# Moving the first input sums, the fetches behind them and the last prepared weights of a one-core decoder layer

## The chip, the cores and the metric

The kernel runs on one core of a Trainium2 chip. The core has a matrix engine (TensorE, PE in the rows; PEld is its weight load), a vector engine (VectorE, DVE), a scalar engine (ScalarE, ACT), a general engine (GpSimd, POOL) and SyncE (SP), which only issues transfers. Each engine works through its own list of instructions in order and waits on semaphores for the others. Transfers are put on a queue by SP, ACT or POOL and run beside the engines.

The metric is the device time of one execution in microseconds (us), the median over several runs. Before the change it is 2637.97 us over three runs (2630.3, 2637.97 and 2639.31).

## What is computed

One decoder layer on 1024 tokens of width 1024, in float32. Only the first of its four parts is touched by most of the change:

```
h = x
f = swiglu(rmsnorm(h, ffn1_pre_g), ffn1_w_gu, ffn1_w_down)   # first feed-forward
h = h + 0.5 * rmsnorm(f, ffn1_post_g)
m = hybrid_mixer(rmsnorm(h, mix_pre_g), ...)                  # attention heads beside a state-space scan
h = h + rmsnorm(m, mix_post_g)
c = memory_cross_attention(rmsnorm(h, xa_pre_g), ...)
h = h + rmsnorm(c, xa_post_g)
f = swiglu(rmsnorm(h, ffn2_pre_g), ffn2_w_gu, ffn2_w_down)   # second feed-forward
h = h + 0.5 * rmsnorm(f, ffn2_post_g)

def swiglu(h, w_gu, w_down):
    g, u = jnp.split(h @ w_gu, 2, axis=-1)
    return (jax.nn.silu(g) * u) @ w_down
```

`D_FF` is 2816, that is 22 column blocks of 128 for the gate and 22 for the up half of `w_gu`.

## The kernel before

**Precision.** A float32 product is made of three matmuls. Each operand is split into a high part (a cast on ACT, L274) and a low part (the rest, a subtraction on DVE, L276), and `mm3` adds high by high, high by low and low by high (L139). So every weight tile costs ACT a cast and DVE a subtraction before TensorE can use it.

**The way up** (`up_phase`). The tokens stand in two halves of 512 columns. The first three gate and up blocks (f = 0 to 2) are plain projections of 24 matmuls each. From f = 3 on, `seven(f)` computes gate and up of both halves at once as seven block products of 12 matmuls each (Strassen's scheme in Winograd's form), 84 matmuls for each f, 19 times. The seven products need sums of input quarters and sums of weight quarters.

- *Input sums.* For k = 0 to 3, `fetch(k)` loads two pairs of quarter rows of x with four transfers on POOL's queue (L686): the pair "ad" into `raw2` (two buffers) and the pair "bc" into `blk`. `steps(k)` then scales the first pair on ACT (L689) and makes three sums on DVE (L699, L702) with their splits (L274, L276) into the tiles S1, S4 and S5. The third load into `raw2` can start only when the sums of k = 0 have read theirs. After these come the differences `B21` (`below`) and `B12` (`again`, `differ`, `last`, L742), which take their data from further loads on POOL's queue.
- *Weight sums.* `pieces(f)` makes five sums of weight quarters on POOL (L762, tile `wc`) and splits seven blocks. For f = 3 each of the five sums is kept in program order.
- *Results.* ACT and DVE take each finished product out of PSUM (L818 to L848); `act_sums` and `pair_sums` make the sums of activations that the way down needs; `act_sums` loads stored activations back over POOL's queue (L621) and adds them on DVE (L628).

**Prepared weights** (`prepare`). Weights of the mixer are split ahead of time while TensorE is busy with the way up. A piece is half a weight tile: one load of 256 KB, a cast on ACT (L212), a subtraction on DVE (L216) and two stores of 256 KB (L226). `prepare_all` queues 64 pieces, those of 20 tiles `ssd` and of the first `QKV` = 12 tiles `qkv`. Fifty-nine of them have times 4100 ns apart from 148000 on and use SP's queue; the last five have times 9000 ns apart from 446000 on, and their loads and stores stand on POOL's queue. The rest of `qkv` (from tile `QKV` on) is prepared in the state-space stage.

**The way down** (`down7`). Again seven block products, over 11 blocks of the contraction, 132 matmuls each. For each block SP loads a weight block (L1018, L1023) and an activation block (L1029), DVE makes a sum (L1032) and splits both (L276). At the end of a product DVE and ACT take the four banks out of PSUM (L1054, L1089) before the next product can add to them.

**What sets the order.** TensorE's order is the program's. Work of the other engines that is not tied to a matmul is put on a list, `self.later`, with a planned time; it is emitted when the planned clock, the sum of the estimated matmul costs, passes this time. What goes through `kp` stays in program order on its engine. The rest a scheduler orders by estimated times and by priority; `urgent` lifts priority. In the running program each engine's list is fixed: an instruction that waits holds back all behind it on the same engine or queue.

Of the kernel before, what the change touches and what calls it, by code (L numbers as in the profile page):

```python
# [10 lines left out]
F32 = mybir.dt.float32  # L11
# [12 lines left out]
NFF = 22  # L24
PLAIN = 3, 4
MIXED = 6
QKV = 12
MEM = 256
EPS = 1e-6

# [17 lines left out]
class Kern:  # L48
# [139 lines left out]
        self.split(hi, lo, raw)  # L188
        return hi, lo

    def prepare(self, names, raw, pairs, times, switch=float("inf")):


        nc = self.nc
        work = []
        for name, i in names:
            hl = tuple(self.tc.dram_tile([P, KT, P], F32R, name=self.nm(n)) for n in ("dwhi", "dwlo"))
            self.ready[name, i] = hl
            work += [(self.ap["w_" + name][i], hl, slice(4 * n, 4 * n + 4)) for n in range(2)]
        raws, parts = {}, {}  # L200

        def queue(n):
            return nc.sync if times[n] < switch else nc.gpsimd

        def load(n):
            pool, tag, bufs = raw[n % len(raw)]
            raws[n] = self.t(pool, [P, 4, P], F32, tag, bufs=bufs)
            self.kp(queue(n).dma_start(out=raws[n], in_=work[n][0][:, work[n][2], :]))

        def high(n):  # L210
            parts[n] = [self.t(pool, [P, 4, P], F32R, tag, bufs=bufs) for pool, tag, bufs in pairs[n % len(pairs)]]
            self.kp(nc.scalar.copy(parts[n][0], raws[n]))  # L212

        def low(n):
            hi, lo = parts[n]
            self.kp(nc.vector.tensor_tensor(out=lo, in0=raws.pop(n), in1=hi.bitcast(F32), op=ALU.subtract))  # L216

        def st0(n):
            store(n, 0)

        def st1(n):
            store(n, 1)

        def store(n, i):
            d, x = work[n][1][i], parts[n][i]
            self.kp(queue(n).dma_start(out=d[:, work[n][2], :].bitcast(F32), in_=x.bitcast(F32)))  # L226

        if len(pairs) > 2:
            steps = ((low, -1, 0), (st0, -2, 0), (st1, -2, 3000), (high, 0, 0), (load, 2, 6000))
        else:  # L230
            steps = ((high, 0, 0), (low, 0, 1200), (load, 2, 2400), (st0, 0, 3000), (st1, 0, 3000))
        times = list(times)[: len(work)]
        assert len(times) == len(work), (len(times), len(work))
        d = times[1] - times[0]
        times = {n: t for n, t in enumerate(times)}
        times.update({-n: times[0] - d * n for n in (1, 2)})
        times.update({len(work) + n: times[len(work) - 1] + d * (n + 1) for n in range(2)})
        for n in sorted(times):
            for f, m, dt in steps:
                if len(pairs) > 2 and times[n] < switch:  # L240
                    dt = 0
                if 0 <= n + m < len(work):
                    self.later.append((times[n] + dt, lambda f=f, m=n + m: f(m)))

# [4 lines left out]
    def prepare_all(self, sp):  # L249
        names = [("ssd", i) for i in [*range(6), *range(12, 26)]] + [("qkv", i) for i in range(QKV)]  # L250
        pairs = [
            ((self.fp, "acc0", None), (self.fp, "acc1", None)), ((self.fp, "rpost", None), (self.tp, "dg", None)),
            ((sp, "bh", None), (sp, "bl", None)),
        ]
        raw = [(sp, "braw", 2), (sp, "braw", 2), (self.xp, "xl0", KT + 1), (self.xp, "xl1", KT + 1)]
        n = 2 * len(names)
        a = [148000 + 4100 * i for i in range(n)]
        k = sum(t < 388000 for t in a)
        self.prepare(names, raw, pairs, a[:k] + [446000 + 9000 * i for i in range(n - k)], 418000)

    def wsrc(self, name, i):
        return self.ready[name, i] if (name, i) in self.ready else self.ap["w_" + name][i]
# [306 lines left out]
    def up_phase(self, sp, sp2, wgu, gpre, act_d, bank, load, plain, sizes, rw=None, begin=None):  # L569

        nc = self.nc
        NFT, NWC, NBLK = sizes
        first_seven = PLAIN[0 if begin else 1]
# [8 lines left out]
        if begin:  # L582
            x = sums(F32)
# [163 lines left out]
        def at(t, f, *args):  # L747
            self.later.append((t, lambda: f(*args)))


        def pieces(f):

            G, U = (load(wgu[2 * f + i], [P, KT, P]) for i in range(2))
# [2 lines left out]
            for a, b, op in (  # L756
# [3 lines left out]
                if b is not None:  # L760
                    t = self.t(sp if begin else sp2, [P, 4, P], F32, "wc", bufs=NWC)
                    inst = nc.gpsimd.tensor_tensor(out=t, in0=a, in1=b, op=op)  # L762
                    if begin and f == first_seven:
                        self.tc.keep_in_program_order(inst)
                    a = t
                n = self.nblk = (self.nblk + 1) % (6 + NBLK)
# [101 lines left out]
            )):  # L868
                homes["ca", k] = homes["bd", k] = x
        for k in range(4):  # L870
            at(t0 + dt * k, fetch, k)
            for n, f in enumerate(steps(k)[: 4 if begin else 5]):
                at(t0 + dt * (k + 1) + 1500 * n, f)

        def gate(w, hh):
            t, ps = ft(), self.proj_now(w, hh)
# [10 lines left out]
        if begin:  # L887
# [10 lines left out]
            for hh in range(2):  # L898
# [6 lines left out]
                t = ts[hh]  # L905
# [1298 lines left out]
    def run(self):  # L2204
        nc, tc, ap = self.nc, self.tc, self.ap
        with tc.tile_pool(name="const", bufs=1) as cp, tc.tile_pool(name="state", bufs=1, reuse_waits="tile") as xp, \
# [54 lines left out]
            def begin(step):  # L2261
                if step < 0:
                    warm()
                elif step == 0:
                    load_x(0)
                elif step == 1:
                    consts()
                    norm_x(0, 8500, 13500)
                else:
                    load_x(1)  # L2270
                    norm_x(1, 22000, 25500)

            self.kv_d = [[tc.dram_tile([P, 4, MEM], F32R, name=f"kv{h}{n}") for n in range(2)] for h in range(4)]
            self.h = [[ap["xT"][d, :, hh * H : (hh + 1) * H] for d in range(KT)] for hh in range(2)]
# [110 lines left out]
```

## Time and profile before

| | before |
|---|---|
| median of three runs | 2637.97 us (2630.3 to 2639.31) |
| profiled execution, its own time | 2634.21 us |
| its span | 2632.4 us |
| mean granted TensorE clock | 0.994 of full speed |
| DVE busy | 1990.6 us (76%) |
| ACT busy | 1291.9 us (49%) |
| POOL busy | 589.4 us (22%) |
| read from and written to memory | 466.4 MB, 177 GB/s over the span |

The profiled execution is one execution of the same program under the profiler; its span is the part between the first and the last instruction. Shares of the span say little here: TensorE is busy nearly always. What matters is the few places at which it isn't, and for each the instruction that it waits for and what stands ahead of that one on its engine.

### The profile page before, as it was taken

Reading aid. Unit: us, or ns where it says so; the run is one execution under the profiler, and the core shown is the slowest. Engines: PE = TensorE matmul, PEld = TensorE weight load, DVE = VectorE, ACT = ScalarE, POOL = GpSimd, SP = SyncE. Lnnn points to the kernel's source line nnn. Section 1 sums busy time; section 2 is a strip of 40 time slices with the busy share of each in tenths; the row PEclk is TensorE's granted clock in tenths of the full one; section 3 lists DMA queues with packets and bytes.
Section 4 is the critical chain, followed back from the end, with each engine's and each line's share of the span. In section 5 each row is a group of like instructions: output and inputs, shape, how many; then the busy total and the mean of one; then the engine's idle time right before and its main releaser. Section 6 shows DMA issues by size and latency. Waiting matters only on the chain.

```text
span 2632.4 us, 36830 instructions
## 1 busy us (share of the span) xinstructions
PE 2586.2 (98%) x12850; PEld 2153.1 (82%) x12850; DVE 1990.6 (76%) x3044; ACT 1291.9 (49%) x2300; POOL 589.4 (22%) x696
## 2 busy tenths in 40 slices
PE   9899999989999999999999999999999999999999
PEld 7688888878777778888888897888878888888887
DVE  6778887768779875777777787767566888777777
ACT  6434443545356664555555555346554433333553
POOL 2555554010100001111111110101011555552000
PEclk9899999999999999999999999999999999999999
DMA  6458887664655516555555556537658453326554
GB/s 227 162 179 293 288 285 259 220 224 142 241 204 188 180 58 207 164 163 141 149 138 134 168 155 230 195 137 248 211 172 294 158 176 116 101 96 228 188 172 152
DMA packets 214314, 489.82 MB, mean 186 GB/s; under 512 B 26544, under 2 KB 35120, under 8 KB 214128
## 3 DMA queue, kind: packets, MB, share of 16 engines
q1 hardware_dynamic: 165920, 374.98, 43.1%
q0 software_dynamic: 24880, 70.01, 8.8%
q10 hardware_dynamic: 23328, 42.48, 4.3%
q8 instruction: 101, 1.65, 0.3%
q14 instruction: 85, 0.70, 0.1%
HBM read 327.46 MB, written 138.94 MB: 177 GB/s over the span
## 4 chain that ended last, share of the span: by engine, by line
PE 86%; DVE 6%; DMA 2%; issue 2%; ACT 2%; POOL 0%; SPq 0%; DVEq 0%; ACTq 0%; POOLq 0%
PE mm L139 45%; PE dn L139 33%; PE z L139 2%; PE tr L142 2%; PE y L139 1%; PE ms L142 1%; PE ms L139 1%; PE seg L139 1%; DMA oraw<-mix 1%; DVE nb L1771 1%; DVE wlo L276 1%; DMA raw<-in_w_dn 1%; PE st L139 0%; DVE xl L276 0%; DVE whi L276 0%
## 5 line engine op out<-in xcount | busy, mean ns | idle before, releaser
L139 PE MATMUL mm<-xh,whi 128*128 128x512 f32 x1320 | 522.1, 405 | 6.8 <-DVE whi L276 2.8
L139 PE MATMUL mm<-xh,wlo 128*128 128x512 f32 x1272 | 488.9, 392 | 0.0
L139 PE MATMUL mm<-xl,whi 128*128 128x512 f32 (+1 forms) x1252 | 487.3, 389 | 1.2 <-DVE xl L276 0.9
L139 PEld LDWEIGHTS mm<-xh,whi 128*128 128x128 f32 x1320 | 249.1, 189 | 49.4 <-issue 3.8
L139 PEld LDWEIGHTS mm<-xh,wlo 128*128 128x128 f32 x1272 | 239.1, 188 | 52.4 <-DVE wlo L276 0.4
L139 PEld LDWEIGHTS mm<-xl,whi 128*128 128x128 f32 x1252 | 236.5, 189 | 35.6 <-DVE xl L276 1.8
L1771 DVE TENSOR_TENSOR_SCAN nb<-nb,begin 128x128 f32<-128x128 f32 (+7 forms) x128 | 171.5, 1352 | 52.1 <-ACT nb L1767 51.6
L1767 ACT ACTIVATE nb<-z,scale 128x128 f32<-128x128 f32 (+2 forms) x192 | 107.8, 580 | 77.7 <-PE z L139 77.5
L276 DVE TENSOR_TENSOR wlo<-wraw,whi 128x1024 fp32r<-128x1024 f32 x70 | 85.5, 1221 | 54.8 <-ACT whi L274 48.4
L274 ACT CAST whi<-wraw 128x1024 fp32r<-128x1024 f32 (+1 forms) x87 | 83.8, 964 | 81.1 <-PE mm L139 55.2
L1788 POOL DMA_DIRECT2D mix<-sq x64 | 52.8, 825 | 228.6 <-DVE sq L1786 176.2
L670 ACT ACTIVATE ft<-ft 128x512 f32<-128x512 f32 x88 | 55.5, 632 | 96.1 <-DVE ft L669 95.5
L139 PE MATMUL dn<-xh,wlo 128*128 128x512 f32 x296 | 101.4, 390 | 0.6 <-DMA wlo<-dwlo 0.6
L762 POOL TENSOR_TENSOR wc<-raw,wraw 128x512 f32<-128x512 f32 x55 | 79.4, 1443 | 57.9 <-DVE blk L276 22.8
L762 POOL TENSOR_TENSOR wc<-wraw,raw 128x512 f32<-128x512 f32 x56 | 79.4, 1418 | 51.0 <-DVE whi L276 15.9
L276 DVE TENSOR_TENSOR atl<-tr,ath 128x512 fp32r<-128x512 f32 (+1 forms) x108 | 67.9, 632 | 30.0 <-ACT ath L274 29.6
L849 POOL TENSOR_TENSOR ft<-ft,e 128x512 f32<-128x512 f32 x37 | 59.8, 1616 | 121.4 <-DVE e L848 53.5
L139 PE MATMUL mm<-ath,v 128*128 128x256 f32 x320 | 85.9, 291 | 0.4 <-ACT sq L1785 0.2
L274 ACT CAST ath<-tr 128x512 fp32r<-128x512 f32 (+1 forms) x108 | 58.8, 546 | 55.4 <-PE tr L142 51.0
L139 PE MATMUL dn<-xh,blk 128*128 128x512 f32 x264 | 85.2, 389 | 0.0
L139 PE MATMUL dn<-hl,whi 128*128 128x512 f32 x288 | 76.0, 397 | 9.1 <-ACT F L1089 9.1
L274 ACT CAST wlo<-wc 128x512 fp32r<-128x512 f32 x79 | 49.1, 621 | 71.3 <-PE dn L139 21.9
(586 smaller groups left out, 6799.4 us busy)
## 6 DMA issues: line engine op xcount, KB each, us to landing
whi<-dwhi SPq DMA_DIRECT2D x82, 512.0 KB, 3.6
wlo<-dwlo SPq DMA_DIRECT2D x82, 512.0 KB, 4.8
wraw<-in_w_gu SPq DMA_DIRECT2D x43, 512.0 KB, 4.0
dwhi<-bh SPq DMA_DIRECT2D x75, 256.0 KB, 4.1
dwlo<-bl SPq DMA_DIRECT2D x75, 256.0 KB, 4.0
raw<-in_w_gu SPq DMA_DIRECT2D x37, 512.0 KB, 4.2
wraw<-xs SPq DMA_DIRECT2D x56, 256.0 KB, 3.0
xs<-ft ACTq DMA_DIRECT2D x54, 256.0 KB, 3.8
```

Source lines behind the costliest of these rows:

```text
L139: self._pe(self.nc.tensor.matmul(out, lhsT, rhs, start=start, stop=stop, skip_group_check=self.more), cost)
L142: self._pe(self.nc.tensor.transpose(out, src, self.ident if ident is None else ident), 109.0)
L274: self.kp(self.nc.scalar.copy(hi, src))
L276: self.nc.vector.tensor_tensor(out=lo, in0=src, in1=hi.bitcast(F32), op=ALU.subtract)
L670: nc.scalar.activation(t, t, AF.Silu)
L762: inst = nc.gpsimd.tensor_tensor(out=t, in0=a, in1=b, op=op)
L849: nc.gpsimd.tensor_tensor(out=t1, in0=t1, in1=e, op=ALU.mult)
L1767: nc.scalar.activation(nb[:, s0:s1], z[:, 0:n], AF.Sigmoid, scale=sc[:, i : i + 1])
L1771: nc.vector.tensor_tensor_scan(out=nb[:, 0:Wd][:, ::-1], data0=nb[:, 0:Wd][:, ::-1], data1=begin[:, S - Wd : S][:, ::-1], initial=0.0, op0 ...
L1788: nc.gpsimd.dma_start(out=self.mix_d[p][a * 64 : a * 64 + 64, csl], in_=o, accum_op=ALU.add)
```

## The change

Five edits.

1. `steps(0)`, the scaling and the three sums of the first pair, is emitted with raised priority (`soon`) and with times from 5000 ns behind its fetch on, 300 ns apart.
2. The fetches for k = 1 to 3 get the planned offsets 7000, 8000 and 13500 in place of 6000, 12000 and 18000, and their steps 9500, 17000 and 23000 in place of 12000, 18000 and 24000. The two small matmul groups of the second half's norm move to the planned times 24000 and 27500, from 22000 and 25500.
3. Of the five weight sums of f = 3 only the first, `G0 + G1`, is kept in program order.
4. All prepared pieces have times 3900 ns apart from 148000 on and use SP's queue; there are no late pieces and no pieces on POOL's queue. The two stores of a piece stand in one step.
5. `QKV` is 11, so `prepare_all` has 62 pieces, and the two pieces of `qkv` tile 11 go to the state-space stage, in front of the 24 that are there.

```diff
-QKV = 12
+QKV = 11
...
-    def prepare(self, names, raw, pairs, times, switch=float("inf")):
+    def prepare(self, names, raw, pairs, times):
...
-        def queue(n):
-            return nc.sync if times[n] < switch else nc.gpsimd
...
-            self.kp(queue(n).dma_start(out=raws[n], in_=work[n][0][:, work[n][2], :]))
+            self.kp(nc.sync.dma_start(out=raws[n], in_=work[n][0][:, work[n][2], :]))
...
-        def store(n, i):
-            d, x = work[n][1][i], parts[n][i]
-            self.kp(queue(n).dma_start(out=d[:, work[n][2], :].bitcast(F32), in_=x.bitcast(F32)))
+        def store(n):
+            for d, x in zip(work[n][1], parts.pop(n)):
+                self.kp(nc.sync.dma_start(out=d[:, work[n][2], :].bitcast(F32), in_=x.bitcast(F32)))
 
         if len(pairs) > 2:
-            steps = ((low, -1, 0), (st0, -2, 0), (st1, -2, 3000), (high, 0, 0), (load, 2, 6000))
+            steps = ((low, -1, 0), (store, -2, 0), (high, 0, 0), (load, 2, 0))
...
-                if len(pairs) > 2 and times[n] < switch:
-                    dt = 0
...
-        a = [148000 + 4100 * i for i in range(n)]
-        k = sum(t < 388000 for t in a)
-        self.prepare(names, raw, pairs, a[:k] + [446000 + 9000 * i for i in range(n - k)], 418000)
+        self.prepare(names, raw, pairs, [148000 + 3900 * i for i in range(n)])
...
+        def now(f):
+            f()
+
+        def soon(f):
+            with self.urgent():
+                f()
...
-                    if begin and f == first_seven:
+                    if begin and f == first_seven and a is G0 and b is G1:
                         self.tc.keep_in_program_order(inst)
...
         for k in range(4):
-            at(t0 + dt * k, fetch, k)
+            t, u, d = (t0 + dt * k, t0 + dt * (k + 1), 1500)
+            if begin:
+                t, u, d = ((0, 5000, 300), (7000, 9500, 1000), (8000, 17000, 1500), (13500, 23000, 1500))[k]
+                t, u = t0 + t, t0 + u
+            at(t, fetch, k)
             for n, f in enumerate(steps(k)[: 4 if begin else 5]):
-                at(t0 + dt * (k + 1) + 1500 * n, f)
+                at(u + d * n, soon if begin and k == 0 else now, f)
...
-                    norm_x(1, 22000, 25500)
+                    norm_x(1, 24000, 27500)
```

The edits shift the lines: rows of the kernel before at L699, L702, L276, L348 and L376 stand at L686, L689, L263, L335 and L363 in the changed one, POOL's weight sums (L762) at L756, its other work (L823, L849) at L817 and L843, and the residual loads (L389) at L376.

DVE's list in the first 50 us, before, from the place right behind the sums of squares of the second half's norm (`acc`, none of which stands below) and the first sum of k = 0, `bl_492`. `bh_506` and `bl_517` are the other two sums of k = 0, `S` the splits of all three, `wlo` splits of plain weight tiles, `cpre` the norm of the second half, `ft` gate values.

```order
L276 TENSOR_TENSOR wlo_661<-wraw_658,whi_660 128x1024
L348 RECIPROCAL cpre_112_346<-cpre_112_346 128x4
L276 TENSOR_TENSOR S_116_361<-bl_492,S_116_361 128x512
L276 TENSOR_TENSOR wlo_667<-wraw_664,whi_666 128x1024
L669 TENSOR_TENSOR ft_463<-mm_464,rpre_113_347 128x512
L702 SCALAR_TENSOR_TENSOR bh_506<-blk_441,params_78,raw_134_438 128x512
L884 TENSOR_TENSOR ft_463<-ft_463,mm_503 128x512
L276 TENSOR_TENSOR S_120_365<-bh_506,S_120_365 128x512
L702 SCALAR_TENSOR_TENSOR bl_517<-blk_441,params_78,raw_134_438 128x512
```

The changed kernel, from the first sum of k = 0 (`bl_476`) to the first plain weight split:

```order
L686 TENSOR_TENSOR bl_476<-raw_134_438 128x512
L363 TENSOR_TENSOR acc_104_323<-acc_104_323,sq_108_334 128x512
L363 TENSOR_TENSOR acc_104_323<-acc_104_323,sq_109_337 128x512
L263 TENSOR_TENSOR S_116_361<-bl_476,S_116_361 128x512
L689 SCALAR_TENSOR_TENSOR bh_481<-blk_441,params_78,raw_134_438 128x512
L363 TENSOR_TENSOR acc_104_323<-acc_104_323,sq_110_340 128x512
L363 TENSOR_TENSOR acc_104_323<-acc_104_323,sq_111_343 128x512
L263 TENSOR_TENSOR S_120_365<-bh_481,S_120_365 128x512
L689 SCALAR_TENSOR_TENSOR bl_486<-blk_441,params_78,raw_134_438 128x512
L263 TENSOR_TENSOR wlo_663<-wraw_660,whi_662 128x1024
L335 RECIPROCAL cpre_112_346<-cpre_112_346 128x4
```

All three sums of k = 0 now stand ahead of the weight split `wlo` and ahead of the gate values `ft_463`; the last of them, the last reader of the first `raw2` buffer, no longer stands behind two results of TensorE. The sums of squares of the second half now stand between them, the last ones three places later than before.

POOL's list in the way down, before. The `dwhi` and `dwlo` stores belong to the last of the late pieces (five loads and eight more stores of such pieces stand above), the loads of L389 fetch the residual of the first half.

```order
L226 DMA dwhi_656<-bh_5043 128x512
L226 DMA dwlo_657<-bl_5044 128x512
L226 DMA dwhi_656<-acc_1147_5123 128x512
L226 DMA dwlo_657<-acc_1148_5124 128x512
L389 DMA xl_1243_5651<-in_xT 128x512
L389 DMA xl_1248_5680<-in_xT 128x512
```

POOL's list in the changed kernel around the same residual loads (now L376); `sq` and `ft` are the last work of the way up.

```order
L843 TENSOR_TENSOR ft_4149<-ft_4149,e_4103 128x512
L817 TENSOR_TENSOR sq_941_4201<-sq_941_4201,sq_940_4200 128x512
L843 TENSOR_TENSOR ft_4291<-ft_4291,e_4263 128x512
L376 DMA xl_1235_5633<-in_xT 128x512
L376 DMA xl_1240_5662<-in_xT 128x512
```

No transfer of a prepared piece is left between the last work of the way up and the loads of the residual. On DVE's list the late subtractions (L216) between the sums of the way down are gone likewise; the rows around them keep their order, but for two pairs of neighbours that change places.

More of the change, by code (lines that the diff above doesn't have):

```diff
@@ L216, in low @@
             self.kp(nc.vector.tensor_tensor(out=lo, in0=raws.pop(n), in1=hi.bitcast(F32), op=ALU.subtract))
[L218 to L222, printed above, removed]
-        def store(n, i):
-            d, x = work[n][1][i], parts[n][i]
-            self.kp(queue(n).dma_start(out=d[:, work[n][2], :].bitcast(F32), in_=x.bitcast(F32)))
+        def store(n):
+            for d, x in zip(work[n][1], parts.pop(n)):
+                self.kp(nc.sync.dma_start(out=d[:, work[n][2], :].bitcast(F32), in_=x.bitcast(F32)))
         if len(pairs) > 2:
-            steps = ((low, -1, 0), (st0, -2, 0), (st1, -2, 3000), (high, 0, 0), (load, 2, 6000))
+            steps = ((low, -1, 0), (store, -2, 0), (high, 0, 0), (load, 2, 0))
         else:
-            steps = ((high, 0, 0), (low, 0, 1200), (load, 2, 2400), (st0, 0, 3000), (st1, 0, 3000))
+            steps = ((high, 0, 0), (low, 0, 1200), (load, 2, 2400), (store, 0, 3000))
         times = list(times)[: len(work)]
```

## The prediction

> **What bounds the kernel now.** I read the page first, then who waits for whom on PE, then a table of stretches, then PE's order of time at the places that these name.
>
> ```profile
> span 2632.4 us, 36830 instructions
> PE 2586.2 (98%) x12850; PEld 2153.1 (82%) x12850; DVE 1990.6 (76%) x3044; ACT 1291.9 (49%) x2300; POOL 589.4 (22%) x696
> PE dn L139 <- ACT F L1089: 9.1, 1, 9.1
> PE mm L139 <- DVE e L828: 5.4, 2, 4.7
> PE mm L139 <- DVE whi L276: 2.8, 1, 2.8
> ```
>
> PE is the bound. The change neither adds nor removes a matmul, so all it can win is time in which PE stands still or runs slowly. The first line of the page gives 2632.4 - 2586.2 = 46 us of idle PE; three waits of one instance each make up 16.6 us of it. The stretches of 10 us (us; then busy time and instructions of PE, PEld, DVE, ACT, POOL; granted clock; DMA share; GB/s) show where:
>
> ```profile
> 80.00:90.00 10.00, 6.22 (x17) 4.29 (x15) 5.60 (x7) 2.21 (x5) 4.87 (x5) 0.68 0.38 132
> 100.00:110.00 10.00, 9.21 (x39) 7.33 (x40) 10.00 (x13) 3.54 (x6) 6.29 (x5) 1.00 0.02 4
> 120.00:130.00 10.00, 5.34 (x16) 3.97 (x15) 6.70 (x11) 1.85 (x3) 3.47 (x4) 0.73 0.75 256
> 240.00:250.00 10.00, 10.00 (x45) 8.27 (x45) 10.00 (x14) 4.22 (x8) 5.96 (x4) 1.00 0.73 232
> 550.00:560.00 10.00, 3.06 (x7) 2.49 (x8) 5.66 (x10) 3.09 (x6) 0.00 (x0) 0.56 0.53 194
> ```
>
> A full stretch holds 45 matmuls; these hold 17, 39, 16 and 7. Between 140 and 540 us PE is full throughout, as at 240, even where DVE is. So there are three holes: at 81 to 102 and 121 to 132 (start of the seven products) and at 548 to 562 (way down). The change touches all three.
>
> **First hole, the sums in front.** PE's order of time (start, duration) and the chain of waits (the two with a count at the end):
>
> ```profile
> 81.63 0.50 PE L139 MATMUL mm<-xh,whi 128*128 128x512 f32 x1 [1.00 <-ACT whi L274]
> 85.14 1.22 PE L139 MATMUL mm<-xh,whi 128*128 128x512 f32 x2 [2.77 <-DVE whi L276]
> 102.33 2.89 PE L139 MATMUL dn<-S,wlo 128*128 128x512 f32 x12
> 147.95 8.16 PE dn L139 x36
> 85.14 4.65 PE mm L139 x10
> ```
>
> Undisturbed matmuls come every 8.16 / 36 = 0.227 us. PE was free at 81.63 - 1.00 = 80.63; five products, 60 matmuls, later it is at 102.33, and 60 x 0.227 = 13.6, so 8.1 us are lost here. What is late is DVE:
>
> ```profile
> 46.40 0.74 DVE L702 SCALAR_TENSOR_TENSOR bl<-blk,params,raw 128x512 f32<-128x512 f32 x1
> 47.69 1.06 POOL L686 DMA_DIRECT2D raw<-in_xT  x2 [31.25 <-DVE bl L702]
> 65.80 0.69 DVE L276 TENSOR_TENSOR S<-bl,S 128x512 fp32r<-128x512 f32 x1 [3.07 <-ACT S L274]
> 83.81 0.68 DVE L884 TENSOR_TENSOR ft<-ft,mm 128x512 f32<-128x512 f32 x1
> 84.40 1.28 DVE L276 TENSOR_TENSOR whi<-wc,whi 128x512 fp32r<-128x512 f32 x2
> 90.95 0.69 DVE L276 TENSOR_TENSOR wlo<-wc,wlo 128x512 fp32r<-128x512 f32 x1 [5.26 <-ACT wlo L274]
> ```
>
> The third sum of k = 0 ran at 46.40; POOL's next loads waited 31 us for it, so the data for k = 2 came late; DVE stood for 3.07 us at 65.8 and then reached L884 at 83.81, 3.2 us after PE had its operand ready, and the low half of the first block behind it.
>
> With the change that third sum stands in front of the weight split and the gate values. Counting DVE's new list on from the gate product ahead of it (about 32.0 before) with 0.69 to 0.74 us each and the casts between, it ends near 39, 8 us earlier, and the loads for k = 2 follow. The sums of k = 1 stay where results of PE hold them, so k = 3 gains only about 1 us of its load. The 3.07 us at 65.8 go, since k = 2's data are there and the cast for S now stands ahead of the scaling that waited for a load. I put DVE at the gate product of 83.81 some 3 us sooner, that is when PE delivers (about 81.1). The low half then ends near 82.3; PE waits some 1.2 us instead of 1.00 + 2.77, and isn't slowed after it. The end of the first product moves from 89.8 to 84.7, and with it ACT's read of that bank, the cast behind it and DVE's split at 90.95: 5 us. From there DVE is busy without a break to 115 us (the row 100 to 110 shows 10.00), so everything behind moves by these same 5 us, no more.
>
> *The clock* has its share in this. The ten matmuls after the second wait took 4.65 us, 0.465 each, twice 0.227: 2.4 us on top of the wait; the granted clock of that stretch is 0.68.
>
> **Second hole.**
>
> ```profile
> 126.20 5.39 PE L139 MATMUL mm<-S,wlo 128*128 128x512 f32 x12 [4.66 <-DVE e L828]
> 118.33 6.46 DMA dg<-act
> ```
>
> L828 stands on DVE behind an addition (L628) that waits for the stored activations, loaded over POOL at 116.7 to 118.3 behind POOL's own work for DVE. It hangs on the same DVE chain, which moves by the 5 us, as does PE's arrival. I leave the 4.7 us as they are: no gain, no loss. **Term: -5.0 us** from both holes. Bounds: 0 if k = 3's load sets the end as before, -8.1 if all of the first hole closes and the load's place moves too.
>
> What this delays: three DVE instructions of 0.7 us come ahead of the last squares of the second half's norm, 2 us. Its two matmul groups are moved back by 2000 ns on purpose, nine or ten matmuls later in PE's list (2.3 us), which covers it; without this cover it costs up to 2 us once. The weight split behind it is 2.6 us later, for weights that PE reaches near 48 us. The weight sums that lose their kept order only swap one L762 with L823 on POOL, 1.7 us at most and 1 us ahead of its reader: 0.
>
> **Third hole, the late pieces.**
>
> ```profile
> 543.61 0.54 POOL L226 DMA_DIRECT2D dwlo<-acc  x1 [3.62 <-DVE acc L216]
> 544.14 2.66 POOL L389 DMA_DIRECT2D xl<-in_xT  x5
> 546.68 7.00 DMA raw<-in_w_dn
> 553.77 0.69 DVE L1032 TENSOR_TENSOR cb<-raw,xl 128x512 f32<-128x512 f32 x1 [5.31 <-DMA raw<-in_w_dn]
> 555.58 0.68 DVE L1054 TENSOR_TENSOR ft<-dn,F 128x512 f32<-128x512 f32 x1
> 556.94 5.10 PE dn L139 x12
> ```
>
> PE ends the third product at 547.8 and may go on when ACT (L1089) has emptied a bank, behind DVE's L1054. That stands behind the sum of a weight block whose load, issued at 546.68, took 7.00 us: five residual loads of 256 KB had gone out in one burst at 544.14, because POOL held them behind the store of the last late piece. Loss: 9.14 + (5.10 - 12 x 0.227) = 11.5 us. Without late pieces the burst can't stand there. Whether the wait goes wholly is answered by the second way down (2410 us on), the same loop without pieces. Loads there and here (count, KB, median us to landing), and PE's first four products there:
>
> ```profile
> raw<-in_w_dn SPq DMA_DIRECT2D x10, 256.0 KB, 4.5
> raw<-in_w_dn SPq DMA_DIRECT2D x13, 256.0 KB, 2.7
> 2409.94 119.71 PE dn L139 x528
> ```
>
> 528 matmuls in 119.71 us is 0.227 each: not one wait over all four products. So I take the whole: **term: -11.5 us**. Bounds: -4.3 if only this landing falls from 7.00 to 2.7, and DVE arrives 4.3 us sooner; -11.5 at the other end.
>
> The Trainium skill, "TensorE: Matmul & The Clock Gate", section "Part 1: The HAM clock gate", has the array at half clock after an idle window of about 3.4 us, until one busy window of the same length. By it a cold window costs half of 3.4, an estimate of 1.7 us for each of the two long holes against 2.4 in the rows; the third term would be 10.8 and the sum 0.7 us less; the trace has half speed too, but longer, and I go by the rows.
>
> **What comes in place.** The way up gets 62 pieces for 59, each with one cast, one subtraction and three transfers:
>
> ```profile
> 528.66 0.69 DVE L216 TENSOR_TENSOR dg<-braw,rpost 128x512 fp32r<-128x512 f32 x1
> SPq L226 <- DVE dg L216: 36.8, 13, 7.7
> 530.67 5.34 DMA wraw<-in_w_dn
> 900.00:920.00 20.00, 20.00 (x121) 15.78 (x121) 18.14 (x36) 12.26 (x24) 0.00 (x0) 1.00 0.39 144
> ```
>
> Three more subtractions are 2.1 us of DVE over 280 us beside a PE that waits for nothing there: 0; with the cover gone 2.1. Their 0.77 MB each go over SP's queue, in which the weight loads of the way up stand too; SP's stores wait up to 7.7 us there. I take 0 and carry the other end as a rival. The burst of residual loads can now come when the way up frees their tiles, near 458 us, 1.3 MB ahead of loads that have five blocks of lead: 0, or up to one landing of 5.34 less the usual 2.7, 2.6 us. Two more pieces in the state-space stage are 1.4 us of DVE where it is busy 18 of 20 us and PE always: 0 to 1.4; I take +0.5.
>
> **Sum** against the profiled execution's own 2634.2 us: -5.0 - 11.5 + 0.5 = -16.0, 2618.2. The median of the three runs is 3.8 us above that execution; part of this scatter will be in such waits. I add half of it: **2620 us**.
>
> **Rivals.**
> - *Only the way down gains.* The sums of k = 1 and k = 3 still hang on PE and on loads at 56 us, and all that is won for k = 2 is lost again by 80 us. Against it: DVE's 3.07 us wait, which has a cause that the change removes. 2634.2 - 11.5 + 0.5 + 1.9 = 2625.
> - *The wait of the way down stays in part.* L1054 still stands behind the same sum of a block; for it: the row 546.68 is issued only when DVE frees the buffer. Against it: the second way down. 2634.2 - 5.0 - 4.3 + 0.5 + 1.9 = 2627.
> - *Slower: SP's queue in the way up.* The weight loads L528 now stand one to four rows further back among the stores of pieces that come 5% more often, and each row may wait for DVE. If the weights of each of 16 column blocks come 2 us too late, this costs 32 us: 2620 + 32 = 2652. It decides from 1 us each, which eats the 16 us. For it: DVE at 10.00 in 240 to 250. Against it: no wait of PE at all in those 400 us, and little more work.
> - *It doesn't do what it says*: the priority moves k = 0, but DVE reaches L884 no sooner, and the burst of residual loads hits the start of the way down: 2636.
> - *More than forecast*: the whole first hole and part of the second, 2613.
>
> **Chances.** Forecast 0.54; only the way down 0.14; in part 0.10; SP's queue 0.12; nothing 0.05; more 0.05. What a measurement of this kernel can tell from no change is about 0.5%, 13 us: 2624.8 to 2651.2. Faster takes the forecast (0.52 of it), the better case and a little of the two at 2625 and 2627 (0.07): 0.64. Slower is SP's queue: 0.12. The rest, 0.24, is the same. The range for 8 of 10 leaves out SP's queue and the edges: 2610 to 2637; the forecast's own is 2614 to 2625.
>
> **What would show it.** Right: no PE wait over 2 us between 540 and 570 us, landings of in_w_dn near 2.7 us, the third sum of k = 0 before 40 us, the first wait for `whi` near 1 us, PE's 102.33 near 97. Wrong: a clock under 0.9 in that stretch; a PE wait for `whi`, `wlo` or `blk` between 140 and 440 us; a new wait near 460; DVE's L884 still after 83.

## The result and the profile after

The changed kernel took 2621.43 us (median of 8 runs, 2616.84 to 2628.6), the kernel before beside it 2634.47 us (8 runs, 2630.3 to 2640.1): 13.0 us less, a ratio of 0.995 with a 95% interval of 0.9934 to 0.9966. The forecast was 2620 us. One execution of this study was slow: one of run 7 took 7204.9 us at a granted clock of 0.352 and stays out of its ratio. In the profiled execution (2623.80 us) the page's first line, the waits of PE and the stretches that the prediction showed now read:

```profile
span 2622.0 us, 36842 instructions
PE 2582.7 (98%) x12850; PEld 2150.6 (82%) x12850; DVE 1990.4 (76%) x3044; ACT 1291.3 (49%) x2300; POOL 583.1 (22%) x681
```

```profile
PE mm L139 <- DVE e L822: 5.5, 2, 4.7
PE mm L139 <- DVE xl L1937: 2.6, 1, 2.6
PE mm L139 <- DVE whi L263: 1.7, 1, 1.7
```

```profile
80.00:90.00 10.00, 8.33 (x38) 6.55 (x37) 6.81 (x10) 5.24 (x11) 5.81 (x4) 1.00 0.31 104
100.00:110.00 10.00, 10.00 (x45) 8.28 (x45) 10.00 (x12) 4.07 (x7) 6.98 (x5) 1.00 0.29 105
120.00:130.00 10.00, 8.49 (x26) 6.79 (x27) 9.44 (x15) 3.58 (x6) 3.60 (x3) 0.66 0.67 229
550.00:560.00 10.00, 10.00 (x45) 8.27 (x45) 7.91 (x13) 4.07 (x8) 0.00 (x0) 1.00 0.72 217
```

The wait for F in the way down (9.1 us) is gone, and the stretch at 550 us holds 45 matmuls for 7. The stretch at 80 us holds 38 for 17, at full clock. The second hole stands as it was, with its slow clock (0.66). PE's and DVE's order of time at the places of the prediction:

```profile
82.59 0.73 PE L139 MATMUL mm<-xh,whi 128*128 128x512 f32 x2 [1.67 <-DVE whi L263]
97.54 2.91 PE L139 MATMUL dn<-S,wlo 128*128 128x512 f32 x12
121.51 5.47 PE L139 MATMUL mm<-S,wlo 128*128 128x512 f32 x12 [4.74 <-DVE e L822]
38.33 0.75 DVE L689 SCALAR_TENSOR_TENSOR bl<-blk,params,raw 128x512 f32<-128x512 f32 x1
65.13 0.69 DVE L263 TENSOR_TENSOR S<-bh,S 128x512 fp32r<-128x512 f32 x1 [2.38 <-ACT S L261]
81.26 0.67 DVE L882 TENSOR_TENSOR ft<-ft,mm 128x512 f32<-128x512 f32 x1
39.62 1.06 POOL L673 DMA_DIRECT2D raw<-in_xT  x2 [23.55 <-DVE bl L689]
```

The third sum of k = 0 starts at 38.33 for 46.40, the loads for k = 2 leave at 39.62 for 47.69, the gate product stands at 81.26 for 83.81, and the twelve matmuls that stood at 102.33 stand at 97.54: 4.8 us gained. For the way down, two rows of POOL's and DVE's order, the loads there (count, KB, median us to landing, 480 to 570 us), and SP's waits in the way up (140 to 460 us; before, then after):

```profile
456.18 2.70 POOL L376 DMA_DIRECT2D xl<-in_xT  x5
541.86 0.69 DVE L1052 TENSOR_TENSOR ft<-dn,F 128x512 f32<-128x512 f32 x1 [0.29 <-PE dn L139]
```

```profile
raw<-in_w_dn SPq DMA_DIRECT2D x16, 256.0 KB, 2.8
```

```profile
SPq L528 <- POOL wc L762: 60.9, 11, 18.9
```

```profile
SPq L515 <- POOL wc L756: 58.7, 12, 18.7
```

The five residual loads still go in one burst, but at 456 us, and PE waits for nothing behind them. DVE now stands for PE at the end of the third product (0.29 us), and no longer PE for DVE. SP's weight loads wait no longer than before, and between 140 and 540 us no wait of PE is listed.

**Where some came back.** PE's order of all 12850 matmuls gives the start of the same matmul in both traces (times of the kernel before). At 620 us the changed kernel is 16.2 us ahead, at 700 us 17.6, at 1417 us 17.1, and from 1690 us on only 10.4; so it still is in the second way down, which began at 2409.94 us before and now has

```profile
2399.54 119.68 PE dn L139 x528
```

The 6.6 us are lost between 1460 and 1690 us, where attention ends and the next part begins. The waits of PE there (1440 to 1740 us), and one stretch of 20 us with the longest wait; before, then after:

```profile
PE mm L139 <- DVE xl L1939: 1.2, 1, 1.2
```

```profile
1480.00:1500.00 20.00, 18.15 (x109) 15.37 (x108) 15.85 (x25) 11.24 (x25) 3.53 (x9) 1.00 0.73 220
```

```profile
PE mm L139 <- DVE xl L1937: 2.6, 1, 2.6
PE dn L139 <- DMA wlo<-dwlo: 1.8, 1, 1.8
```

```profile
1460.00:1480.00 20.00, 16.61 (x97) 14.05 (x96) 14.56 (x22) 11.44 (x23) 2.09 (x5) 0.91 0.67 177
```

The same wait is 1.4 us longer and the granted clock falls to 0.91 behind it. Whether this belongs to the change is the first question of the experiments.

### The profile page after: what moved, and what is told of

Same layout as the page of the kernel before. It is cut to its first block, busy times and chain, and to the rows that moved or that the text cites. A ratio compares the mean times of both kernels' runs of the same rounds, so it can differ in the third digit from the quotient of the medians.

```text
span 2622.0 us, 36842 instructions
## 1 busy us (share of the span) xinstructions
PE 2582.7 (98%) x12850; PEld 2150.6 (82%) x12850; DVE 1990.4 (76%) x3044; ACT 1291.3 (49%) x2300; POOL 583.1 (22%) x681
## 4 chain that ended last, share of the span: by engine, by line
PE 76%; issue 14%; DVE 5%; DMA 3%; ACT 1%; POOL 0%; DVEq 0%; SPq 0%; POOLq 0%; ACTq 0%
PE mm L139 37%; PE dn L139 33%; PE z L139 2%; PE tr L142 2%; PE ms L142 1%; PE ms L139 1%; DVE nb L1769 1%; DVE wlo L263 1%; DMA wraw<-in_w_gu 1%; DMA oraw<-mix 0%; DMA braw<-in_xT 0%; DMA S<-in_xT 0%; DVE whi L263 0%; DVE xl L263 0%; DMA wlo<-dwlo 0%
## 5 line engine op out<-in xcount | busy, mean ns | idle before, releaser
L263 DVE TENSOR_TENSOR wlo<-wraw,whi 128x1024 fp32r<-128x1024 f32 x70 | 85.4, 1221 | 52.4 <-ACT whi L261 52.1
L756 POOL TENSOR_TENSOR wc<-raw,wraw 128x512 f32<-128x512 f32 x55 | 80.5, 1464 | 57.6 <-DVE blk L263 23.2
L263 DVE TENSOR_TENSOR atl<-tr,ath 128x512 fp32r<-128x512 f32 (+1 forms) x108 | 67.9, 632 | 31.4 <-ACT ath L261 31.0
L756 POOL TENSOR_TENSOR wc<-wraw,raw 128x512 f32<-128x512 f32 x56 | 79.7, 1424 | 52.0 <-DVE whi L263 16.7
L843 POOL TENSOR_TENSOR ft<-ft,e 128x512 f32<-128x512 f32 x37 | 59.5, 1608 | 121.2 <-DVE e L842 46.0
L139 PE MATMUL dn<-xh,whi 128*128 128x512 f32 x240 | 84.0, 394 | 0.0
L139 PE MATMUL mm<-atl,v 128*128 128x256 f32 x320 | 83.0, 282 | 0.7 <-DVE atl L263 0.7
```

What stands on the lines that cost most here:

```text
L139: self._pe(self.nc.tensor.matmul(out, lhsT, rhs, start=start, stop=stop, skip_group_check=self.more), cost)
L263: self.nc.vector.tensor_tensor(out=lo, in0=src, in1=hi.bitcast(F32), op=ALU.subtract)
L843: nc.gpsimd.tensor_tensor(out=t1, in0=t1, in1=e, op=ALU.mult)
```

## The experiments

All times are medians, ratios against runs of the kernel before on the same chip, whose medians there were 2636.6 to 2637.4 us.

**1. The start alone.** Edits 1 to 3 put into the kernel before (the lines of the diff shown above for `soon`, the fetch times, `G0`, `norm_x`), `prepare` untouched.

> The kernel before with edits 1 to 3 alone (first pair in front, fetch times, one weight sum kept), prepared pieces as before. Theory A, the two gains stand apart: the start gains what the changed kernel gained there, about 4.8 us (the 12 matmuls dn<-S,wlo that stood at 102.33 stand near 97.5), the second hole stays at 4.7 us, and the way down keeps its wait of 9.1 us for F. Time 2634.5 - 4.8 = 2630, ratio 0.998. Rival B, what the changed kernel gives back between 1490 and 1690 us (some 6.5 us in its profile) hangs on the start being early: then the total is no better than before, 2634. Rival C, the start's gain needs the new times of the pieces: 102.33 stays.

2632.26 us, ratio 0.9982 (0.9973 to 0.9991).

```profile
97.19 2.89 PE L139 MATMUL dn<-S,wlo 128*128 128x512 f32 x12
```

```profile
PE dn L139 <- ACT F L1100: 8.4, 1, 8.4
```

The start gains its 5.1 us alone and the way down keeps its wait: theory A holds. In this profile, too, 6.4 us are lost again between 1430 and 1740 us; the median says that this is not so on the whole, since it is 4.7 us below that of the kernel before.

**2. The pieces alone.** Edits 4 and 5, the start as before.

> The kernel before with edits 4 and 5 alone (all pieces 3900 ns apart on SP's queue, 62 of them), the start as before. Theory A: the first hole stays (102.33), the wait of the way down for F (9.1 us) is gone with the slow matmuls behind it, 11.5 to 12.8 us; nothing new in the way up. Time about 2634.5 - 12 = 2622.5, ratio 0.9954, if what the changed kernel gave back at 1490 to 1690 us is scatter of one execution; rival B, it is the price of the two pieces moved into the state-space stage or of the weights they prepare: then PE loses some 6 us there in this kernel too and the time is near 2628.

2623.13 us, ratio 0.9949 (0.9937 to 0.9962).

```profile
102.55 2.89 PE L139 MATMUL dn<-S,wlo 128*128 128x512 f32 x12
```

No wait for F is listed. The way down gains 11.5 us at this place, and only 0.6 us is given back later (11.9 us ahead at 1421 us, 11.3 at 1724). So the price there isn't that of the two moved pieces: rival B falls.

**3. The changed kernel again**, without an edit.

> The changed kernel once more, beside the kernel before on the chip of the experiments. Its first profile had gained 18.7 us on the kernel before by 700 us and gave back 7 of them between 1460 and 1690 us. Theory A, that is scatter of single executions (waits at places that all kernels share, and the slow clock behind those that grow long): another execution gives back another amount, and the median against the kernel before comes to the sum of the two halves measured alone, -4.7 and -13.9, or 2618.5, ratio 0.993. Rival B, it is systematic, a price of both halves together: again some 7 us given back, ratio 0.995.

2620.0 us, ratio 0.9941 (0.9928 to 0.9953).

```profile
97.83 2.89 PE L139 MATMUL dn<-S,wlo 128*128 128x512 f32 x12
```

The same program gave back 3.5 us between 1460 and 1690 us this time, for 6.6. Measured in the same way over the 13 profiles of this study beside that of before, it is 0.5 to 9.9 us, 4.2 on average: the profile of before happened to be favourable at these waits. It is scatter, and it is a good part of why the difference of two profiles (10.4 us) was less than that of the medians in this run (16.6 us).

The first hole scatters too. Six profiles keep the old start (before and runs 2, 7, 8, 9 and 10); their engines have the same order there, and the matmuls of 102.33 stand at 99.32 to 103.23 us, 101.9 on average. With edits 1 to 3 four profiles (changed kernel, runs 1, 3 and 11) have them at 97.19 to 97.83, 97.5 on average: a gain of 4.4 us, to which the median of run 1 (4.7 us) fits.

**4. Edit 1 alone** (the kernel before, with this, and with `now` and `soon` as in the diff above).

```diff
             at(t0 + dt * k, fetch, k)
+            t, u, d, g = t0 + dt * k, t0 + dt * (k + 1), 1500, now
+            if begin and k == 0:
+                u, d, g = t0 + 5000, 300, soon
             for n, f in enumerate(steps(k)[: 4 if begin else 5]):
-                at(t0 + dt * (k + 1) + 1500 * n, f)
+                at(u + d * n, g, f)
```

> The kernel before with edit 1 alone (the first pair's sums with raised priority, 300 ns apart, 5000 behind the fetch). Theory A, of the prediction: the place of the third sum carries the gain of the start, because POOL's loads for k = 2 wait for it: those loads at 40 in place of 47.7 us, L884 near 81, and the dn<-S,wlo of 102.33 near 97.5 (4.8 us). Rival B, the order of the later fetches and steps carries it: under 2 us gained here.

2629.99 us, ratio 0.9981 (0.9971 to 0.9991).

```profile
39.58 1.07 POOL L686 DMA_DIRECT2D raw<-in_xT  x2 [23.06 <-ACT cpre L347]
52.42 1.06 POOL L686 DMA_DIRECT2D raw<-in_xT  x2 [10.72 <-issue]
95.17 2.89 PE L139 MATMUL dn<-S,wlo 128*128 128x512 f32 x12
119.44 5.49 PE L139 MATMUL mm<-S,wlo 128*128 128x512 f32 x12 [5.06 <-DVE e L835]
```

Edit 1 carries the whole gain, and more than the whole change: 7.2 us at the first hole against the profile of before, 6.7 against the average of the six, with no wait for `whi` left there. 0.8 of it goes again at the second hole, whose wait is longer (5.06 for 4.66). With it alone the loads for k = 3 leave at 52.42; in the changed kernel they leave at

```profile
55.20 1.06 POOL L673 DMA_DIRECT2D raw<-in_xT  x2 [13.46 <-issue]
```

because DVE makes the last sum of k = 1, which reads their buffer, at 53.91 there and at 51.13 here.

**5. The changed kernel without edit 1.**

```diff
-                t, u, d = ((0, 5000, 300), (7000, 9500, 1000), (8000, 17000, 1500), (13500, 23000, 1500))[k]
+                t, u, d = ((0, 6000, 1500), (7000, 9500, 1000), (8000, 17000, 1500), (13500, 23000, 1500))[k]
...
-                at(u + d * n, soon if begin and k == 0 else now, f)
+                at(u + d * n, now, f)
```

> The changed kernel without edit 1: the first pair's steps stand 6000 behind the fetch and 1500 ns apart, without priority; all the rest is the changed kernel's. Theory A: without the third sum in front the loads for k = 2 leave at 46 to 48 us as before, and the start falls back to the times of the kernel before: dn<-S,wlo near 102.3, some 4.8 us slower than the changed kernel. Rival B, the new fetch times and steps carry the gain: it stays near 97.5.

2624.22 us, ratio 0.9959 (0.9944 to 0.9974).

```profile
50.35 1.06 POOL L673 DMA_DIRECT2D raw<-in_xT  x2 [33.82 <-ACT whi L261]
101.89 2.93 PE L139 MATMUL dn<-S,wlo 128*128 128x512 f32 x12
```

The loads for k = 2 leave later than ever, and 101.89 lies among the six profiles of the old start: no gain that one profile could tell from scatter is left. Edits 2 and 3 win nothing there by themselves, and beside edit 1 they cost some 2 us (95.17 in run 4 against 97.19 to 97.83).

**6. The norm groups back** at their old times.

```diff
-                    norm_x(1, 24000, 27500)
+                    norm_x(1, 22000, 25500)
```

> The changed kernel with the two norm groups back at 22000 and 25500. Edit 1 alone had brought the dn<-S,wlo of 102.33 to 95.2, edits 1 to 3 together only to 97.2 to 97.5: some 2 us are lost to edit 2 or 3. Theory A, the moved norm loses them: the second half's gate values wait for its scale (DVE's first ft of that half at 44.8, behind ACT), and what DVE does behind them is late; with the norm back the place comes to 95.5 and DVE's L882 of the end of the plain blocks is done before 80.6. Rival B, the fetch and step times of k = 1 to 3 lose them (their sums stand some 3 us later on DVE than with edit 1 alone): it stays at 97.5.

2620.28 us, ratio 0.9938 (0.9922 to 0.9954).

```profile
54.09 1.06 POOL L673 DMA_DIRECT2D raw<-in_xT  x2 [12.14 <-issue]
96.89 2.89 PE L139 MATMUL dn<-S,wlo 128*128 128x512 f32 x12
121.75 5.49 PE L139 MATMUL mm<-S,wlo 128*128 128x512 f32 x12 [5.65 <-DVE e L822]
```

0.65 us of the 2 come back at the first hole in this one profile, and the second wait takes them (5.65 us): no gain in all. The loads for k = 3 leave 1.1 us sooner of the 2.8 between the changed kernel and run 4. So theory A may hold for a third of it; the rest lies with the fetch and step times or edit 3, which I didn't part from each other.

**7. The late pieces closer together**, one number in the kernel before.

```diff
-        self.prepare(names, raw, pairs, a[:k] + [446000 + 9000 * i for i in range(n - k)], 418000)
+        self.prepare(names, raw, pairs, a[:k] + [446000 + 6000 * i for i in range(n - k)], 418000)
```

> The kernel before with one number changed: the five late pieces stand 6000 ns apart in place of 9000, still late, still on POOL's queue. Theory A, the wait of the way down comes from the burst of residual loads that POOL held behind the last late store: that store now ends some 12 to 15 us sooner, the residual loads go out one by one, the block's landing falls from 7.0 to some 3 us and the wait of 9.1 us for F goes: about 2634.5 - 11.5 = 2623, ratio 0.996. Rival B, late pieces cost what they carry (their subtractions on DVE, 0.77 MB each on the queues) wherever they stand in that stretch: a wait of over 5 us for F stays, time 2630 or more.

2633.74 us, ratio 0.999 (0.9981 to 0.9999).

```profile
529.60 2.65 POOL L389 DMA_DIRECT2D xl<-in_xT  x5
553.72 1.65 PE L139 MATMUL dn<-hl,whi 128*128 128x512 f32 x3 [6.98 <-ACT F L1089]
```

Theory A falls as I had put it: the residual loads are free 14.5 us sooner, but go in a burst all the same, and PE waits 7.0 us in place of 9.1, as rival B said. Among the loads on `raw` from 520 to 572 us the longest landing is now 8.8 us (7.3 before), and DVE's next sums wait behind it.

**8. No burst.** The residual loads of the first half on ACT's queue, late pieces as they were.

```diff
-    def resid(self, hh, step, start=0):
+    def resid(self, hh, step, start=0, q=None):
...
-            self.kp(self.nc.gpsimd.dma_start(out=self.XL[hh][d], in_=self.h[hh][d]))
+            self.kp((q or self.nc.gpsimd).dma_start(out=self.XL[hh][d], in_=self.h[hh][d]))
...
-                self.resid(0, 3500, 16000)
+                self.resid(0, 3500, 16000, self.nc.scalar)
```

> The kernel before, late pieces and all, with one change: the residual loads of the first half in the first way down are issued by ACT in place of POOL, so that they leave at their planned times, after the stretch in question, and no store of a piece holds them. Theory A, the five residual loads in one burst are what delays the weight block: no burst at 544 us, the landings of in_w_dn between 520 and 555 us come to about 3 us, and PE's wait for F at 548 us (9.1 us) falls under 2 us. Rival B, the late pieces' own loads, stores and subtractions delay it (with the last pieces 12 us sooner and the burst with them the wait was still 7.0 us): a wait of 4 us or more stays. The end of the way down may lose something by ACT's waits for the residual tiles.

2632.94 us, ratio 0.9987 (0.9977 to 0.9996).

```profile
548.13 1.65 PE L139 MATMUL dn<-hl,whi 128*128 128x512 f32 x3 [4.39 <-ACT F L1089]
```

```profile
raw<-in_w_dn SPq DMA_DIRECT2D x8, 256.0 KB, 3.1
```

```profile
DVE cb L1032 <- DMA wraw<-in_w_dn: 8.0, 6, 2.7
```

The burst is worth about half: 4.39 us of 9.14 stay, with landings at 3.1 us (the three profiles that keep both burst and late pieces, before and runs 1 and 4, have 9.14, 8.44 and 8.82). (The rows are PE's order, the loads of 520 to 560 us, and DVE's longest waits of 455 to 548 us.) In that stretch the sums L1032 stand 16.4 us for their loads, in twelve waits (15.9 us in nine in the kernel before); with all late pieces gone (run 2) the waits of L1026, the same line, add up to 6 us.

**9 and 10. What of a late piece it is.** Run 8 with each late piece's stores issued twice:

```diff
-            self.kp(queue(n).dma_start(out=d[:, work[n][2], :].bitcast(F32), in_=x.bitcast(F32)))
+            for _ in range(2 if queue(n) is nc.gpsimd else 1):
+                self.kp(queue(n).dma_start(out=d[:, work[n][2], :].bitcast(F32), in_=x.bitcast(F32)))
```

> The kernel before with residual loads on ACT's queue, as in the run of that name, and each late piece's two stores issued twice (10 more transfers of 256 KB). With the burst away PE's wait for F at 548 us was still 4.4 us. Theory T, the late pieces' transfers slow the weight loads: the wait grows to 7 us or more. Theory D, their subtractions stand on DVE between the sums of the weight blocks, which hold the buffers of the next loads: it stays between 3.5 and 5.5 us.

and run 8 with its subtraction done three times:

```diff
-            self.kp(nc.vector.tensor_tensor(out=lo, in0=raws.pop(n), in1=hi.bitcast(F32), op=ALU.subtract))
+            raw = raws.pop(n)
+            for _ in range(3 if queue(n) is nc.gpsimd else 1):
+                self.kp(nc.vector.tensor_tensor(out=lo, in0=raw, in1=hi.bitcast(F32), op=ALU.subtract))
```

> The kernel before with residual loads on ACT's queue, and each late piece's subtraction done three times on DVE (10 more of 0.69 us, the same result). Theory D (DVE's time between the sums): the wait of 4.4 us grows by a good part of 6.9 us, to 8 to 11.5 us. Theory T (the transfers): it stays under 5.5 us.

One execution each, 2635.21 and 2632.85 us. The wait, first with the stores doubled, then with the subtractions tripled:

```profile
552.85 1.65 PE L139 MATMUL dn<-hl,whi 128*128 128x512 f32 x3 [4.07 <-ACT F L1090]
```

```profile
551.98 1.65 PE L139 MATMUL dn<-hl,whi 128*128 128x512 f32 x3 [3.74 <-ACT F L1091]
```

Neither grows. The landings did get longer with more stores (from 500 to 560 us `wraw<-in_w_dn` 4.0 us for 3.2), and the wait didn't follow. So theory T fails in the one run and theory D in the other, as they were put. Neither suspect is cleared by this: with the subtractions tripled DVE stands 9.9 us for its loads in place of 16.4, so the added ones fell into time in which it waited anyway, and from 485 to 548 us `raw` and `wraw` of in_w_dn land in 3.6 and 3.9 us in run 8, but in 2.8 and 2.7 in the changed kernel. Beside these the late pieces' loads on POOL's queue and their casts on ACT are left. What makes up the 4.4 us stays open.

**11. The second hole.** The changed kernel, the first sums of activations moved into the first of the seven-product blocks.

```diff
-            if later_sums and (f in (4, 5) if begin else f > 6 and f % 2):
-                act_sums(later_sums.pop(0), self.clock)
+            if later_sums and (f in (3, 5) if begin else f > 6 and f % 2):
+                act_sums(later_sums.pop(0), self.clock + (12000 if f == 3 else 0))
```

> The changed kernel with one more move: the loads of the stored activations for the first of the sums of activations, and these five sums, are planned in the first of the seven-product blocks (12000 ns into it) in place of the second. Theory A, the second hole (PE waits 4.7 us for DVE's e, then 12 matmuls at half clock, 2.7 us) is DVE standing for these loads, issued only at 111.9 and landed at 119.5: with loads 10 us earlier the wait goes, -7.4 us against the changed kernel, 2614, ratio to the kernel before 0.992. Rival B, DVE is full from 90 to 110 us, so the five sums (3.4 us) standing earlier push the weight splits behind them and PE waits for those instead: 2 to 4 us of the 7.4 are left as gain. Rival C, the wait for e comes from POOL's subtraction in front of it, which stays: no change, 2621.

2618.09 us, ratio 0.9932 (0.9919 to 0.9944).

```profile
119.16 3.02 PE L139 MATMUL mm<-S,wlo 128*128 128x512 f32 x12 [2.51 <-DVE e L822]
116.67 1.71 POOL L817 TENSOR_TENSOR sq<-sq,sq 128x512 f32<-128x512 f32 x1
118.42 0.69 DVE L822 TENSOR_TENSOR e<-sq,mm 128x512 f32<-128x512 f32 x1 [1.15 <-POOL sq L817]
```

PE waits 2.51 us for 4.74, and the twelve matmuls behind it take 3.02 us for 5.47, near full clock: at the same matmul later on (200 us) this kernel is 4.7 us ahead of the changed one. That is one profile; the median is 1.9 us under that of run 3, and the intervals overlap. The row speaks for theory A, by two thirds of its 7.4 us; what is left is rival C, POOL's subtraction, which stands behind a weight sum.

**12. What the runs point to.** Edit 1, the pieces of edits 4 and 5, and the move of run 11; edits 2 and 3 left out.

> What the runs so far say is best: edit 1, the pieces of edits 4 and 5, and the first sums of activations planned in the first seven-product block; edits 2 and 3 left out. Theory A, the parts add up: start -6.6 us, second hole -5, way down -12 to -13; medians of the parts against the kernel before give -6.6 - 13.9 - 2 to -5, about 2613, ratio 0.991. Rival B, DVE's list in the first seven-product block is another without edits 2 and 3 and the moved sums cost there what they win: 2617, ratio 0.9925.

2614.08 us (2611.62 to 2620.26), ratio 0.9913 (0.9896 to 0.9929).

```profile
95.10 2.91 PE L139 MATMUL dn<-S,wlo 128*128 128x512 f32 x12
116.65 3.06 PE L139 MATMUL mm<-S,wlo 128*128 128x512 f32 x12 [2.33 <-DVE e L822]
```

The parts add up: at 724 us it is 24.4 us ahead of the kernel before (the changed kernel 17.6). It beats the kernel before clearly; its interval ends where that of the changed kernel in run 3 begins (0.9928).

## Why the prediction came out right, point by point

- *Start, -5.0 us:* 4.8 in the profile, 4.5 at the same place in run 3, 4.4 between the averages. Third sum (38.33, forecast near 39), loads for k = 2 (8.1 us sooner, forecast 8), L884 (81.26, forecast 81.1), no slow matmuls behind the wait for `whi`: all as worked out, and runs 4 and 5 show that edit 1 carries it (the third sum alone, without the two that move with it, was not tried). About half of the term, 2.4 us, was the slow clock behind the wait for `whi`; that the profile of before had it is a matter of the single execution, since run 8 with the same start has none of it (see below). One step was wrong: "The 3.07 us at 65.8 go". A wait of 2.38 us stands at 65.13. What ends both is ACT: its cast for S stands behind the scaling of `braw`, which waits for a load that POOL issues behind those for k = 3. I had put this cast ahead of the scaling; that was so for k = 2 alone, and k = 3's first cast stands there now. The bound that I named, k = 3's load, fits the runs with edit 1: it leaves at 52.42, 54.09 and 55.20 us, and those matmuls stand at 95.17, 96.89 and 97.54 (run 4, run 6, changed kernel). Without edit 1 the order is not so clean (55.97 and 102.33 before, 57.82 and 101.89 in run 5).
- *Edits 2 and 3 at nothing:* wrong by some 2 us. The norm's cover was counted on PE alone; run 6 gives it a third of the loss at most, and the rest is not parted between the fetch and step times and edit 3. That the term came out is luck: two errors met, since edit 1 alone is worth 7.2 us, of which I had claimed 5.
- *Second hole, no gain, no loss:* right (4.74 for 4.66). It hangs on loads of POOL that move with the rest; runs 4 and 6 show that it takes back part of what is won ahead of it.
- *Way down, -11.5 us:* the size is right, 11.5 us at this place in the changed kernel and in run 2. The cause as I put it, the burst behind the late store, is half of it (runs 7 and 8); the other half goes with the late pieces too, but how is open. What saved the term was the comparison with the second way down, which has neither burst nor pieces. My lower bound, -4.3 us for a landing that falls back to normal, is what run 8 gained in that stretch (4.3), where the burst alone went.
- *What comes in place, +0.5 us:* nothing was lost between 620 and 700 us; the lead grew from 16.2 to 17.6 us. From there to 1417 us, where the state-space stage with its two more pieces lies, it shrank by 0.5 (by 0.3 in run 1, which leaves the pieces as they were). SP's queue, the slower rival, shows waits as before and PE none.
- *Scatter, +1.9 us:* right in part. The profile of before was a good execution by 4.2 us at 1460 to 1690 us, so the changed kernel's profile had that much less to show. But the term was half of the 3.8 us by which the median of three runs lay above this profile. The median of eight is only 0.3 us above it, those of the experiments 2.4 to 3.2. So it is partly luck that the time is within 1.4 us of 2620: the change won 13.0 us against the kernel before beside it, where the sum had 16.0 and the forecast against the first median 18.

On the clock: the twelve matmuls behind a wait of 4.74 us took 5.47 us, those behind 2.51 us only 3.02, against 2.72 undisturbed (12 x 0.227). The Trainium skill, "TensorE: Matmul & The Clock Gate", section "Part 1: The HAM clock gate", puts the drop behind an idle window of about 3.4 us, and these two rows agree. Shorter waits close together go either way. In the kernel before, waits of 1.00 and 2.77 us, two matmuls apart, had ten matmuls at half speed behind them; at the same place run 8 waits 0.48 and 2.81 us and has none, and run 10 waits 2.35 and 1.14 us and has them (granted clock from 80 to 92 us: 0.72, 1.00 and 0.72). The second waits of runs 8 and 10, with the two matmuls behind each:

```profile
84.31 0.73 PE L139 MATMUL mm<-xh,whi 128*128 128x512 f32 x2 [2.81 <-DVE whi L276]
84.84 1.22 PE L139 MATMUL mm<-xh,whi 128*128 128x512 f32 x2 [1.14 <-DVE whi L278]
```

The wait of 2.6 us at 1470 us, with a clock of 0.91 in its stretch, is another such place with other short waits close to it. What decides there, no run here shows.

## What to carry to other kernels

When an instruction is moved forward, ask which buffer its last read frees and which queue stands for that buffer: here three sums of 0.7 us moved forward, the last of which frees such a buffer, were worth 7 us of PE. Test each edit of a set of planned times alone; a set may hold one that wins and others that take part of it back. Before tenths of a microsecond of one profile are given to an edit, see how far profiles of one and the same order differ at that place: here 3.9 us. For the size of a stall, a second instance of the same loop without the suspect is a better witness than a story about the suspect, and the story still has to be tested: take away one suspect, and see how much stays.

## What was not expected of the hardware

Ten more stores of 256 KB in the same stretch made the loads of 256 KB land in 4.0 us for 3.2, and PE's wait was no longer (4.07 for 4.39). Five loads of 256 KB in one burst cost PE 4.75 us of wait at 544 us (9.14 less 4.39), and nothing at 456 us, behind which PE waited for nothing. And the price of a wait is not its length: behind 4.74 us the next twelve matmuls took 0.46 us each, behind 2.51 us 0.25, so that 2.2 us less of wait were worth 4.7. Nor does the length alone say whether the clock falls: the same instructions in the same order ran at half speed behind 1.00 and 2.77 us and at full speed behind 0.48 and 2.81.
